# Rotary embedding on one core: float32 from the given tables, x resident in SBUF, plain transfers, and the work shared by VectorE and GpSimd

## Chip, cores, metric

One core of a Trainium2 chip. The metric is device time in microseconds of one execution, lower is better. In the text, HBM is the main memory, SBUF and PSUM are the two memories on the core, VectorE, ScalarE and GpSimd are the engines that compute, and SyncE here only issues transfers. Most executions of one kernel agree within 0.3%.

## The reference

x is 8 x 8 x 1024 x 64 float32 (16.78 MB), the two tables are 1024 x 32 float32 (0.13 MB each).

```python
x_first, x_second = x[..., :32], x[..., 32:]
out_first  = x_first * cos_cached - x_second * sin_cached
out_second = x_first * sin_cached + x_second * cos_cached
```

Everything must be read and written once: 33.56 MB of HBM traffic without the tables. Per output value there are two products and one sum.

## The kernel before

It treats x as 16 spans of 1 MB (128 partitions x 2048 float32). It does not read the tables: it computes sines and cosines on the chip and keeps them as bfloat16. VectorE works in bfloat16. In the first half of the spans ScalarE casts the input and the store casts back; in the second half the load casts and ScalarE casts the output. Casting transfers are issued by GpSimd.

```python
def compute_piece(x16, tt, ot, off, pc):      # all bfloat16, VectorE
    for k in range(2):
        tensor_tensor(out=t4[:, n0:n1, k], in0=x4[:, n0:n1, 1 - k], in1=sinb[:, n0:n1], op=mult)
    tensor_tensor(out=o4[:, n0:n1], in0=x4[:, n0:n1], in1=cb, op=mult)
    tensor_tensor(out=o4[:, n0:n1, 0], in0=o4[..., 0, :], in1=t4[..., 0, :], op=subtract)
    tensor_tensor(out=o4[:, n0:n1, 1], in0=o4[..., 1, :], in1=t4[..., 1, :], op=add)

def emit_piece_a(...):                        # spans 0 to 7
    nc.scalar.copy(out=x16, in_=xt)           # xt came by a plain load
    compute_piece(...)
    nc.gpsimd.dma_start(out=dst, in_=ot)      # bfloat16 -> float32 in the transfer

def emit_piece_b(...):                        # spans 8 to 15, x16 came by a casting load
    compute_piece(...)
    nc.scalar.copy(out=o32, in_=ot)
    nc.scalar.dma_start(out=dst, in_=o32)     # plain store
# ... table stages, pools and piece sizes cut ...
```

Of the kernel before, what the change touches and what calls it, by code (L numbers as in the profile page):

```python
# [11 lines left out]
def kernel(  # L13
# [7 lines left out]
    nc = tc.nc  # L21
    fp32 = mybir.dt.float32
    bf16 = mybir.dt.bfloat16
    int32 = mybir.dt.int32
    TT = mybir.AluOpType
    AF = mybir.ActivationFunctionType
    P = nc.NUM_PARTITIONS
    PI = float(math.pi)
# [3 lines left out]
    BH = b * h  # L32
    chunk_elems = seq * hd

    T_CH = 4
    n_spans = BH // T_CH
    span_elems = T_CH * chunk_elems
    span_free = span_elems // P
    rpp = span_free // hd
    unit = span_free // T_CH  # L40
    nu = rpp // T_CH

    assert seq % rpp == 0 and (rpp * P) % seq == 0

    xf = x.rearrange("b h s d -> (b h s d)")
    of = out.rearrange("b h s d -> (b h s d)")

    const_pool = ctx.enter_context(tc.tile_pool(name="const", bufs=1))
    x32_pool = ctx.enter_context(tc.tile_pool(name="x32", bufs=6))
    x16_pool = ctx.enter_context(tc.tile_pool(name="x16", bufs=8))  # L50
    t_pool = ctx.enter_context(tc.tile_pool(name="t", bufs=4))
    o_pool = ctx.enter_context(tc.tile_pool(name="o", bufs=5))
    o32_pool = ctx.enter_context(tc.tile_pool(name="o32", bufs=4))

    jj = const_pool.tile([P, half], fp32)
    pb_i = const_pool.tile([P, 1], int32)
    pb_m = const_pool.tile([P, 1], int32)
    pb = const_pool.tile([P, 1], fp32)
    pio2 = const_pool.tile([P, 1], fp32)
    freq = const_pool.tile([P, half], fp32)  # L60
    sinb = const_pool.tile([P, rpp, half], bf16)
    cosb = const_pool.tile([P, rpp, half], bf16)
    nj_t = const_pool.tile([P, rpp * half], fp32)
    an_t = const_pool.tile([P, rpp * half], fp32)
    t_t = const_pool.tile([P, rpp * half], fp32)
    ki_t = const_pool.tile([P, rpp * half], int32)
    ar_t = const_pool.tile([P, rpp * half], fp32)

    nc.gpsimd.iota(pb_i, [[1, 1]], base=0, channel_multiplier=rpp)  # L69
    nc.gpsimd.iota(jj, [[1, half]], base=0, channel_multiplier=0,  # L70
                   allow_small_or_imprecise_dtypes=True)
    nc.gpsimd.memset(pio2, PI / 2)
    nc.vector.tensor_scalar(out=pb_m, in0=pb_i, scalar1=seq - 1, scalar2=None,  # L73
                            op0=TT.bitwise_and)
    nc.vector.tensor_copy(out=pb, in_=pb_m)  # L75
    nc.scalar.activation(out=freq, in_=jj, func=AF.Exp, bias=0.0,  # L76
                         scale=float(-math.log(10000.0) / half))

    def emit_table_stage(n0, n1):
        nn = n1 - n0  # L80
        e0, e1 = n0 * half, n1 * half
        nj = nj_t[:, e0:e1]
        an = an_t[:, e0:e1]
        nc.gpsimd.iota(nj.rearrange("p (n j) -> p n j", j=half),  # L84
                       [[1, nn], [0, half]], base=n0,
                       channel_multiplier=0, allow_small_or_imprecise_dtypes=True)
        freq_b = dataclasses.replace(
            freq, ap=[list(freq.ap[0]), [0, nn], list(freq.ap[1])])
        nc.vector.scalar_tensor_tensor(  # L89
            out=an.rearrange("p (n j) -> p n j", j=half),  # L90
            in0=nj.rearrange("p (n j) -> p n j", j=half),
            scalar=pb[:, 0:1], in1=freq_b, op0=TT.add, op1=TT.mult)
        for (shift, tbl) in ((0.0, sinb), (PI / 2, cosb)):
            t = t_t[:, e0:e1]
            ki = ki_t[:, e0:e1]
            arg = ar_t[:, e0:e1]
            nc.vector.tensor_scalar(out=t, in0=an, scalar1=shift,  # L97
                                    scalar2=1.0 / (2 * PI), op0=TT.add, op1=TT.mult)
            nc.vector.tensor_copy(out=ki, in_=t)  # L99
            nc.vector.scalar_tensor_tensor(out=arg, in0=ki, scalar=-2 * PI,  # L100
                                           in1=an, op0=TT.mult, op1=TT.add)
            bias = 0.0 if shift == 0.0 else pio2[:, 0:1]
            nc.scalar.activation(out=tbl[:, n0:n1], in_=arg.rearrange(  # L103
                "p (n j) -> p n j", j=half), func=AF.Sin, bias=bias, scale=1.0)

    cosb4 = dataclasses.replace(
        cosb, ap=[list(cosb.ap[0]), list(cosb.ap[1]), [0, 2], list(cosb.ap[2])])

    def compute_piece(x16, tt, ot, off, pc):
        n0, n1 = off * nu, (off + pc) * nu  # L110
        x4 = x16.rearrange("p (n k j) -> p n k j", k=2, j=half)
        t4 = tt.rearrange("p (n k j) -> p n k j", k=2, j=half)
        o4 = ot.rearrange("p (n k j) -> p n k j", k=2, j=half)
        for k in range(2):
            nc.vector.tensor_tensor(  # L115
                out=t4[:, n0:n1, k, :], in0=x4[:, n0:n1, 1 - k, :],
                in1=sinb[:, n0:n1, :], op=TT.mult)
        cb = dataclasses.replace(
            cosb4, ap=[cosb4.ap[0], [cosb4.ap[1][0], n1 - n0], cosb4.ap[2], cosb4.ap[3]],
            offset=cosb4.offset + n0 * cosb4.ap[1][0])  # L120
        nc.vector.tensor_tensor(out=o4[:, n0:n1], in0=x4[:, n0:n1], in1=cb, op=TT.mult)  # L121
        nc.vector.tensor_tensor(out=o4[:, n0:n1, 0, :], in0=o4[:, n0:n1, 0, :],  # L122
                                in1=t4[:, n0:n1, 0, :], op=TT.subtract)
        nc.vector.tensor_tensor(out=o4[:, n0:n1, 1, :], in0=o4[:, n0:n1, 1, :],  # L124
                                in1=t4[:, n0:n1, 1, :], op=TT.add)

    def emit_piece_a(xt, x16, tt, ot, dst, off, pc):
        fr0, fr1 = off * unit, (off + pc) * unit
        nc.scalar.copy(out=x16[:, fr0:fr1], in_=xt[:, fr0:fr1])  # L129
        compute_piece(x16, tt, ot, off, pc)  # L130
        nc.gpsimd.dma_start(out=dst[:, fr0:fr1], in_=ot[:, fr0:fr1])  # L131

    def emit_piece_b(x16, tt, ot, o32, dst, off, pc):
        fr0, fr1 = off * unit, (off + pc) * unit
        compute_piece(x16, tt, ot, off, pc)
        nc.scalar.copy(out=o32[:, fr0:fr1], in_=ot[:, fr0:fr1])  # L136
        nc.scalar.dma_start(out=dst[:, fr0:fr1], in_=o32[:, fr0:fr1])

    def span_arrs(i):
        base = i * span_elems  # L140
        src = xf[base:base + P * span_free].rearrange("(p m) -> p m", p=P)
        dst = of[base:base + P * span_free].rearrange("(p m) -> p m", p=P)
        return src, dst

    nh = n_spans // 2

    src0, dst0 = span_arrs(0)
    xt0 = x32_pool.tile([P, span_free], fp32, name="xt")
# [74 lines left out]
```

## Time and profile before

| | before |
|---|---|
| time, median of 3 | 90.06 us (90.05 to 90.18) |
| span of the profile that the prediction read | 89.7 us |
| busy: VectorE, ScalarE, GpSimd | 75%, 41%, 15% |
| three DMA queues together | 97.4% of 16 engines' span |

The span runs from the first instruction to the last one on the core. "DMA" in the slices is the mean busy share of the 16 DMA engines in tenths, "GB/s" what they moved.

### The profile page before, as it was taken

The page shows a single profiled execution, that of the slowest core. Times are in us where ns is not written, and L with a number is a line of the kernel's source. Part 1 is how long each engine was busy: PE and PEld are TensorE (multiplying, and loading weights), DVE is VectorE, ACT ScalarE, POOL GpSimd, SP SyncE. Part 2 cuts the span into 40 slices and gives each one's busy share as a digit, 9 for nine tenths or more (in the row PEclk, how much of TensorE's full clock was granted, in tenths as well). Part 3 has the DMA queues.
Part 4 walks back from the last instruction along what each step waited for, and adds up shares of the span by engine and source line. Part 5 has one row for each costly group of instructions (what it writes and reads, how often), then busy time and mean ns, then how long its engine had stood idle before and what let it go on. Part 6 is the DMA issues. An engine that isn't in the chain of part 4 may idle for free.

```text
span 89.7 us, 286 instructions
## 1 busy us (share of the span) xinstructions
DVE 67.0 (75%) x133; ACT 36.4 (41%) x31; POOL 13.0 (15%) x31
## 2 busy tenths in 40 slices
DVE  1000898999999999999999495735959999999000
ACT  5133499989985000000000614400616285747200
POOL 7000000050420420201409722000000000000000
DMA  1999999999998499999599999999999999999991
GB/s 32 246 371 426 427 420 420 438 424 365 389 415 294 184 354 186 416 427 362 208 446 177 331 312 236 316 309 332 318 216 254 339 265 348 405 427 422 409 381 48
DMA packets 6049, 29.37 MB, mean 327 GB/s; under 512 B 672, under 2 KB 928, under 8 KB 3616
## 3 DMA queue, kind: packets, MB, share of 16 engines
q0 software_dynamic: 3024, 12.58, 50.3%
q1 hardware_dynamic: 1440, 8.39, 24.3%
q10 hardware_dynamic: 1584, 8.39, 22.8%
q14 instruction: 1, 0.01, 0.0%
HBM read 16.78 MB, written 16.78 MB: 374 GB/s over the span
## 4 chain that ended last, share of the span: by engine, by line
DVE 35%; DMA 29%; issue 16%; POOL 6%; ACT 5%; SPq 1%; DVEq 0%; POOLq 0%
DMA x<-in_x_dram 19%; DVE tt L115 11%; DMA xt<-in_x_dram 9%; DVE ot L121 9%; DVE ot L122 6%; DVE ot L124 6%; POOL out_dram L131 4%; POOL x L187 2%; ACT x L129 2%; DVE ar_t L100 2%; ACT L103 1%; ACT o L136 1%; ACT sinb L103 0%; SPq L155 0%; SPq L158 0%
## 5 line engine op out<-in xcount | busy, mean ns | idle before, releaser
L136 ACT CAST o<-ot 128x2048 f32<-128x2048 bf16 (+2 forms) x11 | 15.8, 1433 | 39.5 <-DVE ot L124 39.3
L115 DVE TENSOR_TENSOR tt<-x,sinb 128x1024 bf16<-128x1024 bf16 (+2 forms) x44 | 23.3, 540 | 6.3 <-DMA x<-in_x_dram 6.3
L121 DVE TENSOR_TENSOR ot<-x,cosb 128x2048 bf16<-128x2048 bf16 (+2 forms) x22 | 20.2, 928 | 0.0
L129 ACT CAST x<-xt 128x2048 bf16<-128x2048 f32 (+2 forms) x11 | 15.4, 1427 | 6.4 <-DMA xt<-in_x_dram 6.4
L122 DVE TENSOR_TENSOR ot<-ot,tt 128x1024 bf16<-128x1024 bf16 (+2 forms) x22 | 11.8, 540 | 0.1
L124 DVE TENSOR_TENSOR ot<-ot,tt 128x1024 bf16<-128x1024 bf16 (+2 forms) x22 | 11.8, 539 | 0.0
L131 POOL DMA_DIRECT2D out_dram<-ot x11 | 6.0, 545 | 38.4 <-DVE ot L124 38.4
L89 DVE SCALAR_TENSOR_TENSOR an_t<-nj_t,pb,freq 128x256 f32<-128x256 f32 (+1 forms) x3 | 1.6, 570 | 8.1 <-ACT freq L76 8.1
L187 POOL DMA_DIRECT2D x<-in_x_dram x7 | 3.7, 540 | 0.0
L100 DVE SCALAR_TENSOR_TENSOR ar_t<-ki_t,an_t 128x256 f32<-128x256 int32 (+1 forms) x6 | 3.0, 508 | 0.3 <-ACT sinb L103 0.3
L184 POOL DMA_DIRECT2D x<-in_x_dram x3 | 1.6, 537 | 2.6 <-DMA out_dram<-ot 2.0
L99 DVE CAST ki_t<-t_t 128x256 int32<-128x256 f32 (+1 forms) x6 | 1.9, 332 | 0.0
L97 DVE TENSOR_SCALAR t_t<-an_t 128x256 f32<-128x256 f32 (+1 forms) x6 | 1.9, 331 | 0.0
L103 ACT ACTIVATE cosb<-ar_t,pio 128x256 bf16<-128x256 f32 (+1 forms) x3 | 1.6, 573 | 0.4 <-DVE ar_t L100 0.4
L129 ACT ACT_TABLE_LOAD x1 | 1.3, 1283 | 0.7 <-PEq L207 0.7
L103 ACT ACTIVATE sinb<-ar_t 128x256 bf16<-128x256 f32 (+1 forms) x3 | 1.3, 476 | 0.0
L103 ACT ACT_TABLE_LOAD x1 | 1.3, 1283 | 0.0
L84 POOL IOTA nj_t<- 128x256 f32 (+1 forms) x3 | 1.3, 449 | 0.0
L73 DVE TENSOR_SCALAR pb_m<-pb_i 128x1 int32<-128x1 int32 x1 | 0.2, 154 | 1.0 <-POOL pb_i L69 1.0
L76 ACT ACTIVATE freq<-jj 128x32 f32<-128x32 f32 x1 | 0.2, 224 | 0.0
L69 POOL IOTA pb_i<- 128x1 int32 x1 | 0.1, 123 | 0.4 <-PEq L218 0.4
L75 DVE CAST pb<-pb_m 128x1 f32<-128x1 int32 x1 | 0.2, 153 | 0.0
(6 smaller groups left out, 0.6 us busy)
## 6 DMA issues: line engine op xcount, KB each, us to landing
xt<-in_x_dram SPq DMA_DIRECT2D x7, 1024.0 KB, 13.7
out_dram<-ot POOLq DMA_DIRECT2D x6, 1024.0 KB, 5.0
out_dram<-o ACTq DMA_DIRECT2D x6, 1024.0 KB, 8.0
x<-in_x_dram POOLq DMA_DIRECT2D x7, 512.0 KB, 13.2
out_dram<-ot POOLq DMA_DIRECT2D x3, 512.0 KB, 5.1
out_dram<-o ACTq DMA_DIRECT2D x3, 512.0 KB, 5.6
xt<-in_x_dram SPq DMA_DIRECT2D x2, 256.0 KB, 3.7
xt<-in_x_dram SPq DMA_DIRECT2D x1, 512.0 KB, 6.5
```

What stands on the lines that cost most here:

```text
L97: nc.vector.tensor_scalar(out=t, in0=an, scalar1=shift, scalar2=1.0 / (2 * PI), op0=TT.add, op1=TT.mult)
L99: nc.vector.tensor_copy(out=ki, in_=t)
L100: nc.vector.scalar_tensor_tensor(out=arg, in0=ki, scalar=-2 * PI, in1=an, op0=TT.mult, op1=TT.add)
L103: nc.scalar.activation(out=tbl[:, n0:n1], in_=arg.rearrange("p (n j) -> p n j", j=half), func=AF.Sin, bias=bias, scale=1.0)
L115: nc.vector.tensor_tensor(out=t4[:, n0:n1, k, :], in0=x4[:, n0:n1, 1 - k, :], in1=sinb[:, n0:n1, :], op=TT.mult)
L121: nc.vector.tensor_tensor(out=o4[:, n0:n1], in0=x4[:, n0:n1], in1=cb, op=TT.mult)
L122: nc.vector.tensor_tensor(out=o4[:, n0:n1, 0, :], in0=o4[:, n0:n1, 0, :], in1=t4[:, n0:n1, 0, :], op=TT.subtract)
L124: nc.vector.tensor_tensor(out=o4[:, n0:n1, 1, :], in0=o4[:, n0:n1, 1, :], in1=t4[:, n0:n1, 1, :], op=TT.add)
L129: nc.scalar.copy(out=x16[:, fr0:fr1], in_=xt[:, fr0:fr1])
L131: nc.gpsimd.dma_start(out=dst[:, fr0:fr1], in_=ot[:, fr0:fr1])
L136: nc.scalar.copy(out=o32[:, fr0:fr1], in_=ot[:, fr0:fr1])
L187: nc.gpsimd.dma_start(out=x16, in_=src)
```

## The change

The intent: use the given tables in float32, make every transfer plain (no cast, none issued by GpSimd), keep all of x in SBUF and rotate it in place, and split the 16 chunks between VectorE and GpSimd. VectorE's tables and its second product lie in PSUM, so that it has at most one SBUF input and does not compete with GpSimd's reads. Cut to its core:

```diff
-    # tables computed on the chip, bfloat16; casts on ScalarE; casting transfers on GpSimd
+    nc.scalar.dma_start(out=cs[0:Q], in_=cos_cached...)          # Q = 32 partitions
+    nc.scalar.dma_start(out=sn[0:Q], in_=sin_cached...)
+    for c in range(n_ch):                                        # 16 chunks of 1 MB
+        nc.sync.dma_start(out=xt[c], in_=xf[c])
+    for r in range(reps):                                        # 4 groups of 32 partitions
+        nc.scalar.copy(out=csp[r * Q:(r + 1) * Q], in_=cs[0:Q])  # PSUM
+        nc.vector.tensor_copy(out=snp[r * Q:(r + 1) * Q], in_=sn[0:Q])
+    for r in range(1, reps):
+        nc.gpsimd.tensor_copy(out=cs[r * Q:(r + 1) * Q], in_=cs[0:Q])
+    for r in range(1, reps):
+        nc.gpsimd.tensor_copy(out=sn[r * Q:(r + 1) * Q], in_=sn[0:Q])
+    def rotate(eng, q, c, n0, n1, t1, t2, ctab, stab):
+        eng.tensor_tensor(out=a, in0=xr, in1=tab(ctab, n0, n1), op=TT.mult)
+        eng.tensor_tensor(out=s, in0=xr, in1=tab(stab, n0, n1), op=TT.mult)
+        eng.tensor_tensor(out=xr[:, :, 0], in0=a[:, :, 0], in1=s[:, :, 1], op=TT.subtract)
+        eng.tensor_tensor(out=xr[:, :, 1], in0=a[:, :, 1], in1=s[:, :, 0], op=TT.add)
+        q.dma_start(out=of[c]..., in_=xt[c]...)
+    # on_vector: tables csp, snp and product s in PSUM, stores on ScalarE's queue
+    # on_pool:   tables cs, sn and both products in SBUF, stores on SyncE's queue
+    pool_chunks = (1, 4, 7, 10, 13)                              # the other ten: VectorE
+    on_pool(15, 16, R); on_vector(15, 0, 8); on_vector(15, 8, 16)   # last chunk, by rows
```

More of the change, by code (lines that the diff above doesn't have):

```diff
@@ L2 @@
-import dataclasses
-import math
 from contextlib import ExitStack
@@ L7 @@
 import concourse.tile as tile
-from concourse import bass_utils, mybir
+from concourse import mybir
 from concourse._compat import with_exitstack
@@ L22 @@
     fp32 = mybir.dt.float32
-    bf16 = mybir.dt.bfloat16
-    int32 = mybir.dt.int32
     TT = mybir.AluOpType
-    AF = mybir.ActivationFunctionType
     P = nc.NUM_PARTITIONS
-    PI = float(math.pi)
     b, h, seq, hd = x.shape
     half = hd // 2
-    BH = b * h
-    chunk_elems = seq * hd
-    T_CH = 4
-    n_spans = BH // T_CH
-    span_elems = T_CH * chunk_elems
-    span_free = span_elems // P
-    rpp = span_free // hd
-    unit = span_free // T_CH
-    nu = rpp // T_CH
-    assert seq % rpp == 0 and (rpp * P) % seq == 0
@@ L45 @@
-    xf = x.rearrange("b h s d -> (b h s d)")
-    of = out.rearrange("b h s d -> (b h s d)")
-    const_pool = ctx.enter_context(tc.tile_pool(name="const", bufs=1))
-    x32_pool = ctx.enter_context(tc.tile_pool(name="x32", bufs=6))
-    x16_pool = ctx.enter_context(tc.tile_pool(name="x16", bufs=8))
-    t_pool = ctx.enter_context(tc.tile_pool(name="t", bufs=4))
-    o_pool = ctx.enter_context(tc.tile_pool(name="o", bufs=5))
-    o32_pool = ctx.enter_context(tc.tile_pool(name="o32", bufs=4))
-    jj = const_pool.tile([P, half], fp32)
@@ L56 @@
-    pb_i = const_pool.tile([P, 1], int32)
-    pb_m = const_pool.tile([P, 1], int32)
-    pb = const_pool.tile([P, 1], fp32)
-    pio2 = const_pool.tile([P, 1], fp32)
-    freq = const_pool.tile([P, half], fp32)
-    sinb = const_pool.tile([P, rpp, half], bf16)
-    cosb = const_pool.tile([P, rpp, half], bf16)
-    nj_t = const_pool.tile([P, rpp * half], fp32)
-    an_t = const_pool.tile([P, rpp * half], fp32)
-    t_t = const_pool.tile([P, rpp * half], fp32)
-    ki_t = const_pool.tile([P, rpp * half], int32)
@@ L67 @@
-    ar_t = const_pool.tile([P, rpp * half], fp32)
-    nc.gpsimd.iota(pb_i, [[1, 1]], base=0, channel_multiplier=rpp)
-    nc.gpsimd.iota(jj, [[1, half]], base=0, channel_multiplier=0,
-                   allow_small_or_imprecise_dtypes=True)
-    nc.gpsimd.memset(pio2, PI / 2)
-    nc.vector.tensor_scalar(out=pb_m, in0=pb_i, scalar1=seq - 1, scalar2=None,
-                            op0=TT.bitwise_and)
-    nc.vector.tensor_copy(out=pb, in_=pb_m)
-    nc.scalar.activation(out=freq, in_=jj, func=AF.Exp, bias=0.0,
-                         scale=float(-math.log(10000.0) / half))
@@ L79, in emit_table_stage @@
-    def emit_table_stage(n0, n1):
-        nn = n1 - n0
-        e0, e1 = n0 * half, n1 * half
-        nj = nj_t[:, e0:e1]
-        an = an_t[:, e0:e1]
-        nc.gpsimd.iota(nj.rearrange("p (n j) -> p n j", j=half),
-                       [[1, nn], [0, half]], base=n0,
-                       channel_multiplier=0, allow_small_or_imprecise_dtypes=True)
-        freq_b = dataclasses.replace(
-            freq, ap=[list(freq.ap[0]), [0, nn], list(freq.ap[1])])
-        nc.vector.scalar_tensor_tensor(
-            out=an.rearrange("p (n j) -> p n j", j=half),
-            in0=nj.rearrange("p (n j) -> p n j", j=half),
-            scalar=pb[:, 0:1], in1=freq_b, op0=TT.add, op1=TT.mult)
-        for (shift, tbl) in ((0.0, sinb), (PI / 2, cosb)):
-            t = t_t[:, e0:e1]
-            ki = ki_t[:, e0:e1]
-            arg = ar_t[:, e0:e1]
-            nc.vector.tensor_scalar(out=t, in0=an, scalar1=shift,
-                                    scalar2=1.0 / (2 * PI), op0=TT.add, op1=TT.mult)
-            nc.vector.tensor_copy(out=ki, in_=t)
-            nc.vector.scalar_tensor_tensor(out=arg, in0=ki, scalar=-2 * PI,
-                                           in1=an, op0=TT.mult, op1=TT.add)
-            bias = 0.0 if shift == 0.0 else pio2[:, 0:1]
-            nc.scalar.activation(out=tbl[:, n0:n1], in_=arg.rearrange(
-                "p (n j) -> p n j", j=half), func=AF.Sin, bias=bias, scale=1.0)
@@ L106 @@
-    cosb4 = dataclasses.replace(
-        cosb, ap=[list(cosb.ap[0]), list(cosb.ap[1]), [0, 2], list(cosb.ap[2])])
-    def compute_piece(x16, tt, ot, off, pc):
-        n0, n1 = off * nu, (off + pc) * nu
-        x4 = x16.rearrange("p (n k j) -> p n k j", k=2, j=half)
-        t4 = tt.rearrange("p (n k j) -> p n k j", k=2, j=half)
-        o4 = ot.rearrange("p (n k j) -> p n k j", k=2, j=half)
-        for k in range(2):
-            nc.vector.tensor_tensor(
-                out=t4[:, n0:n1, k, :], in0=x4[:, n0:n1, 1 - k, :],
-                in1=sinb[:, n0:n1, :], op=TT.mult)
-        cb = dataclasses.replace(
-            cosb4, ap=[cosb4.ap[0], [cosb4.ap[1][0], n1 - n0], cosb4.ap[2], cosb4.ap[3]],
-            offset=cosb4.offset + n0 * cosb4.ap[1][0])
-        nc.vector.tensor_tensor(out=o4[:, n0:n1], in0=x4[:, n0:n1], in1=cb, op=TT.mult)
-        nc.vector.tensor_tensor(out=o4[:, n0:n1, 0, :], in0=o4[:, n0:n1, 0, :],
-                                in1=t4[:, n0:n1, 0, :], op=TT.subtract)
-        nc.vector.tensor_tensor(out=o4[:, n0:n1, 1, :], in0=o4[:, n0:n1, 1, :],
-                                in1=t4[:, n0:n1, 1, :], op=TT.add)
@@ L127, in emit_piece_a @@
-    def emit_piece_a(xt, x16, tt, ot, dst, off, pc):
-        fr0, fr1 = off * unit, (off + pc) * unit
-        nc.scalar.copy(out=x16[:, fr0:fr1], in_=xt[:, fr0:fr1])
-        compute_piece(x16, tt, ot, off, pc)
-        nc.gpsimd.dma_start(out=dst[:, fr0:fr1], in_=ot[:, fr0:fr1])
-    def emit_piece_b(x16, tt, ot, o32, dst, off, pc):
-        fr0, fr1 = off * unit, (off + pc) * unit
-        compute_piece(x16, tt, ot, off, pc)
-        nc.scalar.copy(out=o32[:, fr0:fr1], in_=ot[:, fr0:fr1])
-        nc.scalar.dma_start(out=dst[:, fr0:fr1], in_=o32[:, fr0:fr1])
@@ L139, in span_arrs @@
-    def span_arrs(i):
-        base = i * span_elems
-        src = xf[base:base + P * span_free].rearrange("(p m) -> p m", p=P)
-        dst = of[base:base + P * span_free].rearrange("(p m) -> p m", p=P)
-        return src, dst
-    nh = n_spans // 2
-    src0, dst0 = span_arrs(0)
-    xt0 = x32_pool.tile([P, span_free], fp32, name="xt")
-    x16_0 = x16_pool.tile([P, span_free], bf16, name="x16")
-    tt0 = t_pool.tile([P, span_free], bf16, name="tt")
-    ot0 = o_pool.tile([P, span_free], bf16, name="ot")
@@ L152 @@
-    nc.sync.dma_start(out=xt0[:, 0:unit], in_=src0[:, 0:unit])
-    emit_table_stage(0, nu)
-    emit_piece_a(xt0, x16_0, tt0, ot0, dst0, 0, 1)
-    nc.sync.dma_start(out=xt0[:, unit:2 * unit], in_=src0[:, unit:2 * unit])
-    emit_table_stage(nu, 2 * nu)
-    emit_piece_a(xt0, x16_0, tt0, ot0, dst0, 1, 1)
-    nc.sync.dma_start(out=xt0[:, 2 * unit:], in_=src0[:, 2 * unit:])
-    emit_table_stage(2 * nu, rpp)
-    emit_piece_a(xt0, x16_0, tt0, ot0, dst0, 2, 2)
-    for i in range(1, nh):
-        src, dst = span_arrs(i)
-        xt = x32_pool.tile([P, span_free], fp32, name="xt")
-        x16 = x16_pool.tile([P, span_free], bf16, name="x16")
-        tt = t_pool.tile([P, span_free], bf16, name="tt")
-        ot = o_pool.tile([P, span_free], bf16, name="ot")
-        nc.sync.dma_start(out=xt, in_=src)
-        pieces = [2, 2] if i == 1 else [T_CH]
-        off = 0
-        for pc in pieces:
-            emit_piece_a(xt, x16, tt, ot, dst, off, pc)
-            off += pc
@@ L175 @@
-    for i in range(nh, n_spans):
-        src, dst = span_arrs(i)
-        x16 = x16_pool.tile([P, span_free], bf16, name="x16")
-        tt = t_pool.tile([P, span_free], bf16, name="tt")
-        ot = o_pool.tile([P, span_free], bf16, name="ot")
-        o32 = o32_pool.tile([P, span_free], fp32, name="o32")
-        if i == n_spans - 1:
-            for (off, pc) in ((0, 2), (2, 1), (3, 1)):
-                fr0, fr1 = off * unit, (off + pc) * unit
-                nc.gpsimd.dma_start(out=x16[:, fr0:fr1], in_=src[:, fr0:fr1])
-                emit_piece_b(x16, tt, ot, o32, dst, off, pc)
-        else:
-            nc.gpsimd.dma_start(out=x16, in_=src)
-            pieces = [2, 2] if i == n_spans - 2 else [T_CH]
-            off = 0
-            for pc in pieces:
-                emit_piece_b(x16, tt, ot, o32, dst, off, pc)
-                off += pc
+    R = 32
@@ new lines @@
+    F = R * hd
+    T = R * half
+    Q = seq // R
+    reps = P // Q
+    n_ch = (b * h * seq) // (R * P)
+    assert seq % R == 0 and P % Q == 0 and Q % 32 == 0
+    xf = x.rearrange("b h s d -> (b h s d)").rearrange(
+        "(c p m) -> c p m", p=P, m=F)
+    of = out.rearrange("b h s d -> (b h s d)").rearrange(
+        "(c p m) -> c p m", p=P, m=F)
+    const = ctx.enter_context(tc.tile_pool(name="const", bufs=1))
+    xp = ctx.enter_context(tc.tile_pool(name="xp", bufs=1))
+    tv = ctx.enter_context(tc.tile_pool(name="tv", bufs=2))
@@ new lines @@
+    tg = ctx.enter_context(tc.tile_pool(name="tg", bufs=1))
+    pt = ctx.enter_context(
+        tc.tile_pool(name="pt", bufs=1, space=bass.MemoryType.PSUM))
+    cs = const.tile([P, T], fp32, name="cs")
+    sn = const.tile([P, T], fp32, name="sn")
+    csp = pt.tile([P, T], fp32, name="csp")
+    snp = pt.tile([P, T], fp32, name="snp")
+    nc.scalar.dma_start(out=cs[0:Q], in_=cos_cached.rearrange("(p n) j -> p (n j)", p=Q))
+    nc.scalar.dma_start(out=sn[0:Q], in_=sin_cached.rearrange("(p n) j -> p (n j)", p=Q))
@@ new lines @@
+    xt = [xp.tile([P, F], fp32, name=f"x{c}") for c in range(n_ch)]
+    for c in range(n_ch):
[7 more added lines that the diff above has]
+        nc.gpsimd.tensor_copy(out=sn[r * Q:(r + 1) * Q], in_=sn[0:Q])
@@ new lines, in rows, with tab @@
+    def rows(t, n0, n1):
+        return t[:, n0 * hd:n1 * hd].rearrange("p (n k j) -> p n k j", k=2, j=half)
+    def tab(t, n0, n1):
+        v = t[:, n0 * half:n1 * half].rearrange("p (n o j) -> p n o j", o=1, j=half)
+        return v.to_broadcast([P, n1 - n0, 2, half])
+    def rotate(eng, q, c, n0, n1, t1, t2, ctab, stab):
+        xr, a, s = rows(xt[c], n0, n1), rows(t1, n0, n1), rows(t2, n0, n1)
+        eng.tensor_tensor(out=a, in0=xr, in1=tab(ctab, n0, n1), op=TT.mult)
+        eng.tensor_tensor(out=s, in0=xr, in1=tab(stab, n0, n1), op=TT.mult)
+        eng.tensor_tensor(out=xr[:, :, 0], in0=a[:, :, 0], in1=s[:, :, 1], op=TT.subtract)
+        eng.tensor_tensor(out=xr[:, :, 1], in0=a[:, :, 1], in1=s[:, :, 0], op=TT.add)
+        q.dma_start(out=of[c][:, n0 * hd:n1 * hd], in_=xt[c][:, n0 * hd:n1 * hd])
@@ new lines, in on_vector, with on_pool @@
+    def on_vector(c, n0=0, n1=R):
+        a = tv.tile([P, F], fp32, name="va")
+        s = pt.tile([P, F], fp32, name="vs")
+        rotate(nc.vector, nc.scalar, c, n0, n1, a, s, csp, snp)
+    def on_pool(c, n0=0, n1=R):
+        a = tg.tile([P, F], fp32, name="ga")
+        s = tg.tile([P, F], fp32, name="gs")
+        rotate(nc.gpsimd, nc.sync, c, n0, n1, a, s, cs, sn)
+    pool_chunks = (1, 4, 7, 10, 13)
+    for c in range(n_ch - 1):
+        if c in pool_chunks:
+            on_pool(c)
+        else:
+            on_vector(c)
@@ L196 @@
+    c = n_ch - 1
+    on_pool(c, 16, R)
+    on_vector(c, 0, 8)
+    on_vector(c, 8, 16)
 _INS = ['x', 'cos_cached', 'sin_cached']
```

## The prediction

> **What bounds the kernel now.** I read the page first: busy shares, the slices, the DMA queues, then the groups with shapes kept apart, then the windows.
>
> ```profile
> DVE 67.0 (75%) x133; ACT 36.4 (41%) x31; POOL 13.0 (15%) x31
> ...
> DMA  1999999999998499999599999999999999999991
> GB/s 32 246 371 426 427 420 420 438 424 365 389 415 294 184 354 186 416 427 362 208 446 177 331 312 236 316 309 332 318 216 254 339 265 348 405 427 422 409 381 48
> ...
> q0 software_dynamic: 3024, 12.58, 50.3%
> q1 hardware_dynamic: 1440, 8.39, 24.3%
> q10 hardware_dynamic: 1584, 8.39, 22.8%
> ...
> HBM read 16.78 MB, written 16.78 MB: 374 GB/s over the span
> ```
>
> No compute engine is near its limit (VectorE 75%), but the 16 DMA engines are busy in nearly every slice, and the three queues' shares add up to 97.4% of 16 engines' span. So the transfers set the time. They move 33.56 MB of HBM traffic, the reference's minimum; only their rate can improve. q0 is the GpSimd-issued queue, whose transfers also cast between float32 and bfloat16: 16.78 MB of HBM traffic (8.39 each way; the page counts 12.58) in 50.3% x 89.7 = 45.1 us of all engines, 372 GB/s. The plain queues do 8.39 MB in 21.8 us (385 GB/s, slow start included) and in 20.5 us (410 GB/s).
>
> The windows show the same in time. Columns: stretch, length, busy us of each engine, clock, DMA share, GB/s.
>
> ```profile
> 4.00:16.00 12.00, 6.23 (x22) 7.77 (x10) 0.00 (x0) 1.00 1.00 406
> ...
> 22.00:50.00 28.00, 27.97 (x44) 6.00 (x4) 8.03 (x16) 1.00 1.00 318
> 50.00:76.00 26.00, 19.62 (x30) 10.49 (x6) 2.06 (x4) 1.00 1.06 299
> 76.00:84.00 8.00, 6.84 (x22) 5.27 (x6) 0.00 (x0) 1.00 1.01 419
> ```
>
> Plain float32 loads alone run at 406 GB/s, plain stores alone at 419; the middle, with casting transfers, shows 299 to 318 although the engines are as busy (part of the drop is only that casts are counted at their smaller side). The ends cost about 2 us before the first packets, and about 2 us between the last heavy slice and the span's end.
>
> **What the Trainium skill says.** (1) "DMA: Bandwidth & Descriptors", section "Measured": a 16 MB load ran at 425 GB/s against about 436 at the fabric; the best slices here (420 to 438) agree. (2) "VectorE: DVE Perf Modes", section "The perf-mode tier table": a two-input elementwise operation runs at twice the base rate in bfloat16 and at the base rate in float32 or with any PSUM operand. The bfloat16 half agrees with this trace: 2048 elements start 1.14 us apart, or 0.53 ns per element plus 0.07 us. No float32 one with two tensors lies in the trace alone to check the other. (3) "SBUF — State Buffer", section "Who interferes with whom": a VectorE instruction with two SBUF inputs contends with GpSimd reads; one with at most one does not. This explains the tables and one product in PSUM. The old trace cannot show it: GpSimd computes nothing there beyond index generation. (4) "GPSIMD Engine Reference", section 3.1: an addition of two 2048-element float32 tensors takes 4497 ns. No row here checks that.
>
> ```profile
> L115 DVE TENSOR_TENSOR tt<-x,sinb 128x1024 bf16<-128x1024 bf16 x24 | 16.3, 686 | 6.3 <-DMA x<-in_x_dram 6.3
> L121 DVE TENSOR_TENSOR ot<-x,cosb 128x2048 bf16<-128x2048 bf16 x12 | 14.6, 1219 | 0.0
> ...
> L129 ACT CAST x<-xt 128x1024 bf16<-128x1024 f32 x3 | 3.0, 1043 | 3.5 <-DMA xt<-in_x_dram 3.5
> ```
>
> **The change, part by part.**
>
> *Removed:* the sine/cosine computation (first product only at 14.7 us in the timeline), both ScalarE casts (about 31 us, beside other work), and all casting DMA. *Added to DMA:* 0.26 MB of tables. Total 33.56 + 0.26 = 33.82 MB. At 413 GB/s, the middle of 406 and 419, that is 81.9 us; with 2 + 2 us for the ends, 85.9 us. This is the DMA floor.
>
> *Start.* By semaphore increments in the old trace, a first 0.25 MB issued at 0.74 us lands between 3.2 and 4.3 us over the engines, and later megabytes every 2.48 us. I put the two tables at 4.5 and 5.2 us (they share the engines with x), x's first chunk at 6, the second at 8.5. ScalarE then makes four PSUM copies of 1024 elements (1.04 us each by its row, plus the waits that the compiled order shows between them): done about 9. VectorE makes four at about 1.2 us from 5.2: done about 10.2 us. GpSimd makes six copies; at 1.0 us each (the 512-element index generation takes 0.62) from 4.5 this would be 10.5, but different partition groups may overlap: I take 9.8.
>
> *VectorE, 10.5 of 16 chunks.* Per chunk two products of 2048 at the base rate and two sums of 1024. Base rate is twice the 0.53 ns: 2048 / 0.96 = 2.13 + 0.07 = 2.20 us; 1024: 1.07 + 0.07 = 1.14. Sum 2 x 2.20 + 2 x 1.14 = 6.68; the order has one self-wait directly behind its producer per chunk, 0.08 us (as the last L122 of the old trace after its L121), and I add 0.08 for PSUM: 6.84. Ten chunks 68.4; the two quarter chunks about 2.0 each: 72.4. End at 10.2 + 72.4 = 82.6. The last 256 KB store then takes about 2.7 us and the span ends 0.85 us after the last landing (88.87 against 89.71 in the old trace): 86.2.
>
> *GpSimd, 5.5 chunks.* 2 x 4.50 + 2 x 2.30 = 13.6 us each, 74.8 in all: end at 84.6; its 512 KB store about 3.2 us, 0.85 more: 88.7.
>
> *Loads* are all issued early, x is never overwritten by another chunk, so compute should wait for data only at the start. Stores come at 1.05 MB per 6.84 us and per 13.6 us, 231 GB/s together, beside the loads on the same DMA engines. GpSimd's stores stand behind all loads in SyncE's order; loads should be through about 60 us, after which some 3 MB of backlog drain within 15 us. The DMA should have slack at the end.
>
> **The path to the end** thus moves from DMA to the later of VectorE (86.2 us span) and GpSimd (88.7), with DMA at 85.9 just behind. Timed runs stood 0.35 us over the span before (90.06 against 89.71), giving 86.5, 89.0 and 86.2. I choose 87.8: the kernel's hand-picked split (a half chunk to GpSimd, the rest in two short stores on VectorE) suggests its author saw the two end together, and GpSimd not late, so I take 1.2 us off the GpSimd sum that rests on a page's figure.
>
> **Rivals.**
> 1. *GpSimd is the end.* If a product takes the page's 4.5 us and waits between dependent GpSimd instructions add 0.3 us a chunk, and the copies run to 11 us, it ends at 11 + 76.5 = 87.5, and the time is 91.9: same or slower. For it: the largest sum of the three. Against: the chosen split. A cold start of GpSimd's library could add to this; the old trace shows such a configuration instruction at 11 ns.
> 2. *DMA stays the bound.* Loads and stores mixed might run below 406; at 390 GB/s (close to the mean of the two plain queues' 385 and 410) 33.82 MB take 86.7 + 4 + 0.35 = 91.1 us: same. For it: DMA is the bound now, and no stretch of the old trace has plain loads beside plain stores. Against: the stretch from 16 to 22 us, mixed, shows 411.
> 3. *PSUM operands or port sharing slow VectorE.* 5% on VectorE gives 3.6 us more, 90 us.
> 4. *GpSimd faster than the page* (4.1 us a product): all three end at 86, a gain of 4 to 5%.
>
> **Range and chances.** The three sums span 86.2 to 89.0; rival 4 and early data take one to two us off, rivals 1 to 3 add two to four: 84.8 to 92.0. Faster by over 2% means below 88.26, just above my value: 0.50. Within 2%: 0.36. Slower (above 91.86), if rivals 1 and 2 come together or GpSimd is well slower than the page: 0.14.
>
> **What would show it right or wrong.** The DMA slices should be full to about 70 us at 400 or more, and fall off after. VectorE rows: 2.2 to 2.3 us for 2048, 1.15 to 1.2 for 1024, first product near 10 us. GpSimd spacing: about 4.5 and 2.3 us, no wait for x after the first chunk. The chain that ended last should run back through GpSimd or VectorE products, not through a load. Wrong would be: VectorE waiting for x in the middle; mixed DMA under 390 GB/s; GpSimd rows far from 4.5 us; VectorE rows stretched while GpSimd runs.

## The result

| | before | after |
|---|---|---|
| time, median of 4 runs | 90.12 us (90.05 to 90.27) | 93.13 us (93.00 to 93.21) |
| ratio | | 1.0318, 95% interval 1.0282 to 1.0354 |
| span of a fast execution | 88.4 us (profiled again later) | 91.1 us |

A ratio here is the mean time of one kernel's fast runs over that of the other's of the same rounds, so not quite the ratio of the medians quoted. The changed kernel is 3.2% slower, and its time lies above the predicted range.

The page of the changed kernel: busy shares, slices, totals.

```profile
DVE 76.3 (84%) x52; ACT 5.3 (6%) x5; POOL 81.5 (89%) x34
...
POOL 0079999999999999999999999999999999999940
DMA  3899999999999999999999999999999911949963
GB/s 54 259 365 358 424 410 432 424 406 435 424 414 435 421 435 424 432 424 417 432 428 435 424 432 424 414 435 428 435 421 435 421 47 47 414 173 410 403 246 149
...
HBM read 17.04 MB, written 16.78 MB: 371 GB/s over the span
```

The DMA engines are no longer busy to the end. They run at 406 to 435 GB/s from 9 until about 73 us and then have holes (two slices of 47). GpSimd (the row POOL) is now busy in nearly every slice. The windows say it in numbers; columns are stretch, length, busy us of VectorE, ScalarE and GpSimd, clock, DMA share, GB/s.

```profile
16.00:40.00 24.00, 23.89 (x14) 0.00 (x0) 23.69 (x9) 1.00 1.01 425
40.00:71.00 31.00, 30.83 (x20) 0.00 (x0) 30.69 (x9) 1.00 1.01 427
71.00:80.00 9.00, 8.97 (x7) 0.00 (x0) 8.92 (x4) 1.00 0.52 218
```

Loads and stores mixed run at 425 to 427 GB/s, where the kernel before had 299 to 318 by the page's count in its middle. That count takes a casting load at its bfloat16 size. In the fast profile of experiment 8 the same stretches show 336 and 300, and with the casting loads' packets counted as float32 373 and 420, together 396, so the rate rose by about 8%. To that extent this part of the intent was met. From 71 to 80 us the DMA engines are half idle while both compute engines are busy all the time. The groups, one shape a row, with busy time and mean ns of one:

```profile
L76 DVE TENSOR_TENSOR vs<-x,snp 128x2048 f32<-128x2048 f32 x10 | 23.0, 2296 | 0.3
L75 DVE TENSOR_TENSOR va<-x,csp 128x2048 f32<-128x2048 f32 x10 | 22.8, 2279 | 0.0
L76 POOL TENSOR_TENSOR gs<-x,sn 128x2048 f32<-128x2048 f32 x5 | 22.6, 4516 | 0.0
L75 POOL TENSOR_TENSOR ga<-x,cs 128x2048 f32<-128x2048 f32 x5 | 22.6, 4515 | 0.4
...
L78 POOL TENSOR_TENSOR x<-ga,gs 128x1024 f32<-128x1024 f32 x5 | 11.7, 2332 | 0.0
L77 POOL TENSOR_TENSOR x<-ga,gs 128x1024 f32<-128x1024 f32 x5 | 11.6, 2324 | 0.4
```

The chain that ended last, in order of time (start, length, what):

```profile
1.17 7.08 DMA sn<-in_sin_cached_dram
...
11.58 4.51 POOL ga L75
...
86.35 1.21 POOL x L78
```

So the end is set thus: GpSimd copies the two tables to its other partitions, begins its first product at 11.58 us, and works without a real pause until 87.56. Its last store and the program's end take 3.56 us more. The chain names the sine table, which landed at 8.26 us, because it came last, but by little: the cosine table landed at 4.94, and GpSimd was busy with its three copies of it until 8.17. The start thus rests on the cosine's landing and on six copies in a row (from the timeline):

```profile
4.99 3.18 POOL L62 COPY cs<-cs 32x1024 f32<-32x1024 f32 x3 [4.55 <-DMA cs<-in_cos_cached_dram]
...
8.31 3.18 POOL L64 COPY sn<-sn 32x1024 f32<-32x1024 f32 x3
```

### The profile page after: what moved, and what is told of

The parts are those of the page before. It is cut to its first block, busy times and chain, and to the rows that moved or that the text cites. A ratio compares the mean times of both kernels' runs of the same rounds, so it can differ in the third digit from the quotient of the medians.

```text
span 91.1 us, 196 instructions
## 1 busy us (share of the span) xinstructions
DVE 76.3 (84%) x52; ACT 5.3 (6%) x5; POOL 81.5 (89%) x34
## 4 chain that ended last, share of the span: by engine, by line
POOL 84%; DMA 8%; issue 2%; POOLq 2%; ACTq 0%
POOL ga L75 27%; POOL gs L76 27%; POOL x L78 14%; POOL x L77 13%; DMA sn<-in_sin_cached_dram 8%; POOL sn L64 3%; POOLq L126 1%; ACTq L51 0%; POOLq L75 0%
## 5 line engine op out<-in xcount | busy, mean ns | idle before, releaser
L75 POOL TENSOR_TENSOR ga<-x,cs 128x2048 f32<-128x2048 f32 (+1 forms) x6 | 24.9, 4155 | 0.5
L76 POOL TENSOR_TENSOR gs<-x,sn 128x2048 f32<-128x2048 f32 (+1 forms) x6 | 24.9, 4155 | 0.0
L76 DVE TENSOR_TENSOR vs<-x,snp 128x2048 f32<-128x2048 f32 (+1 forms) x12 | 24.4, 2029 | 0.4
L75 DVE TENSOR_TENSOR va<-x,csp 128x2048 f32<-128x2048 f32 (+1 forms) x12 | 24.1, 2012 | 0.0
L77 POOL TENSOR_TENSOR x<-ga,gs 128x1024 f32<-128x1024 f32 (+1 forms) x6 | 12.9, 2146 | 0.5
L77 DVE TENSOR_TENSOR x<-va,vs 128x1024 f32<-128x1024 f32 (+1 forms) x12 | 13.0, 1080 | 0.0
L78 DVE TENSOR_TENSOR x<-va,vs 128x1024 f32<-128x1024 f32 (+1 forms) x12 | 12.9, 1079 | 0.0
L78 POOL TENSOR_TENSOR x<-ga,gs 128x1024 f32<-128x1024 f32 (+1 forms) x6 | 12.9, 2152 | 0.0
L60 DVE COPY snp<-sn 32x1024 f32<-32x1024 f32 x4 | 4.9, 1222 | 8.4 <-DMA sn<-in_sin_cached_dram 8.3
L62 POOL COPY cs<-cs 32x1024 f32<-32x1024 f32 x3 | 3.1, 1032 | 4.6 <-DMA cs<-in_cos_cached_dram 4.5
L59 ACT COPY csp<-cs 32x1024 f32<-32x1024 f32 x4 | 4.0, 1008 | 2.1 <-DMA cs<-in_cos_cached_dram 2.0
L64 POOL COPY sn<-sn 32x1024 f32<-32x1024 f32 x3 | 3.1, 1033 | 0.2
```

What stands on the lines that cost most here:

```text
L59: nc.scalar.copy(out=csp[r * Q:(r + 1) * Q], in_=cs[0:Q])
L60: nc.vector.tensor_copy(out=snp[r * Q:(r + 1) * Q], in_=sn[0:Q])
L62: nc.gpsimd.tensor_copy(out=cs[r * Q:(r + 1) * Q], in_=cs[0:Q])
L64: nc.gpsimd.tensor_copy(out=sn[r * Q:(r + 1) * Q], in_=sn[0:Q])
L75: eng.tensor_tensor(out=a, in0=xr, in1=tab(ctab, n0, n1), op=TT.mult)
L76: eng.tensor_tensor(out=s, in0=xr, in1=tab(stab, n0, n1), op=TT.mult)
```

## The experiments

All spans below are of the profiled execution; where rounds were run, the ratio is given. "Gap" is the time of the profiled run minus its span. A run without a ratio is one execution whose state is unknown.

### 1. The sine table first

```diff
-    nc.scalar.dma_start(out=sn[0:Q], in_=sin_cached...)
+    nc.sync.dma_start(out=sn[0:Q], in_=sin_cached...)      # ahead of the loads of x
```

> The sine table goes ahead of x on SyncE's queue instead of second on ScalarE's. Theory A (GpSimd's chain sets the end, and began late because the sine table landed at 8.2 us behind x): both tables land by about 4.5 us, GpSimd's first product starts at about 10.6 instead of 11.6 us, the whole chain and the span move by the same 1 us (91.1 to 90.1), and VectorE starts about 3.5 us earlier without helping. Rival B (DMA or the last stores set the end): the span does not move though GpSimd starts earlier.

Measured: correct, span 90.1, time 92.17 us; ratio to before 1.0187 (1.0117 to 1.0258). Its timeline (start, length, engine, instruction):

```profile
3.74 4.99 DVE L60 COPY snp<-sn 32x1024 f32<-32x1024 f32 x4 [3.74 <-DMA sn<-in_sin_cached_dram]
...
4.08 3.18 POOL L62 COPY cs<-cs 32x1024 f32<-32x1024 f32 x3 [3.64 <-DMA cs<-in_cos_cached_dram]
...
10.58 4.52 POOL L75 TENSOR_TENSOR ga<-x,cs 128x2048 f32<-128x2048 f32 x1
```

The sine table lands at 3.72 instead of 8.26 us, and the cosine table, now with no load of x issued before 1.18 us instead of 0.74, at 4.03 instead of 4.94. GpSimd's first product starts 1.00 us earlier, the span ends 1.05 us earlier. VectorE starts 4.4 us earlier (8.77 against 13.18) and gains nothing for the span. Theory A holds in its main part: GpSimd's chain is the end, and a microsecond at its start is a microsecond at the end. Its reason for the late start does not: 0.91 of the 1.00 us come from the cosine, on which GpSimd waits first, and only about 0.1 from the sine.

### 2. Eight rows from GpSimd to VectorE

```diff
-    on_pool(c, 16, R);  on_vector(c, 0, 8);   on_vector(c, 8, 16)
+    on_pool(c, 24, R);  on_vector(c, 0, 16);  on_vector(c, 16, 24)
```

> Eight rows of the last chunk move from GpSimd to VectorE. Theory A (GpSimd alone is the end): GpSimd ends 8 x 0.43 = 3.4 us earlier (84.1), VectorE 1.7 later (about 86.9), and the span falls by about 0.7 to 1.2 us, VectorE's last store being the end. Rival (VectorE equally late already, or a DMA backlog at the end): no gain or a loss.

Measured: correct, span 91.2, time 93.35 us; ratio to before 1.0316 (1.0256 to 1.0377), no better than without the edit (1.0318). From its timeline:

```profile
83.81 0.72 POOL L78 TENSOR_TENSOR x<-ga,gs 128x256 f32<-128x256 f32 x1
...
86.40 0.41 DVE L78 TENSOR_TENSOR x<-va,vs 128x256 f32<-128x256 f32 x1
```

GpSimd ends at 84.53, 3.0 us earlier; VectorE ends at 86.81, 1.66 later, and is now the end of the chain. The span does not fall, since the tail after the last product grows from 3.56 to 4.4 us. In the trace VectorE's 512 KB and 256 KB stores follow each other within 1.5 us onto DMA engines that are busy just then; that this lengthens the tail was not tested. The size of the gain in theory A was a miss. The two engines were within 2.4 us of balance; shifting rows alone cannot help, only an earlier start or less work can.

### 3. Padding VectorE's instruction stream

The time of the changed kernel stood 2.0 us over its span, where the prediction had taken 0.35. The trace shows an 8 KB instruction transfer after the last instruction, at 93.0 us; the kernel before had one at 24.4 us.

```diff
+    pad = const.tile([P, 128], fp32, name="pad")
+    for i in range(96):
+        nc.vector.memset(pad[:, i:i + 1], 0.0)    # while VectorE waits for the tables
```

> 96 one-element memsets of a scratch tile on VectorE while it waits for the tables, nothing else. The timed 93.1 us stand 2.0 us over the span of 91.1, where the kernel before stands 0.35 over its own. Theory F (an instruction block has to be fetched at the program's end, since the new kernel has few instructions; the trace shows an 8 KB instruction transfer after the end where the kernel before had one at 24.7 us): if VectorE is the engine, the gap falls from 2.0 to about 0.4 us while the span stays 91 to 91.5. Rival G (the gap comes from GpSimd computing, or from PSUM): the gap stays 2.0.

Measured: correct, span 91.1, time 92.89 us, gap 1.77. The instruction transfer moved to 7.6 us, but the gap fell by only 0.25 us. A late instruction transfer goes with 0.2 to 0.3 us (gaps 2.02, 1.94 and 2.06 in the three kernels that show one at the end, 1.77 or 1.78 in nine others; runs 9 and 13 have 2.18 and 2.17 without one at the end, which stays open). It does not explain the rest.

### 4. Transfers only

```diff
-    # table copies, rotate, on_vector, on_pool
+    for c in range(n_ch):
+        q = nc.sync if c in (1, 4, 7, 10, 13) else nc.scalar
+        q.dma_start(out=of[c], in_=xt[c])          # wrong result on purpose
```

> Wrong result on purpose: loads and stores of the changed kernel without any computing (x is written back as it is). The transfers' own floor: theory A expects a span of 82 to 86 us, well under 91, as the slices showed 410 to 435 GB/s with loads and stores mixed; a DMA bound would show 89 or more. For the gap between time and span: theory F (few instructions) expects about 2 us here too; rival G (GpSimd computing or PSUM causes it) expects 0.4.

Measured: span 84.5, time 86.27 us, gap 1.78. Its windows, columns as before without VectorE and ScalarE:

```profile
16.00:40.00 24.00, 0.00 (x0) 1.00 1.01 427
40.00:71.00 31.00, 0.00 (x0) 1.00 1.01 427
```

The transfers of the changed kernel need 84.5 us of span, 6.6 less than it takes and 3.9 less than the 88.4 of the kernel before. So the plain transfers did lower the DMA floor, if the span of the kernel before is taken as its own floor (its queues fill 98.0% of it; no run took the computing out of that kernel); the changed kernel does not reach the new one. The gap is 1.78 us without any computing, so GpSimd computing or PSUM do not cause it.

### 5 to 7. What the gap goes with

```diff
# gp_touch: the changed kernel
-    nc.scalar.dma_start(out=cs[0:Q], in_=cos_cached...)
+    nc.gpsimd.dma_start(out=cs[0:Q], in_=cos_cached...)
# no_tables: transfers only, without the two table loads (wrong result on purpose)
# before_tables: the kernel before, plus
+    nc.sync.dma_start(out=tabs[:, 0], in_=cos_cached...)   # read by nobody
+    nc.sync.dma_start(out=tabs[:, 1], in_=sin_cached...)
```

> The changed kernel with one transfer, the cosine table, issued by GpSimd instead of ScalarE. The padding run and the transfers-only run refuted an instruction fetch and GpSimd computing as the cause of the 1.8 to 2.0 us between span and time. Theory H (a kernel in which GpSimd issues no transfer pays it; the kernel before had 22 such): the gap falls to about 0.4 us here. Rival I (it goes with reading the two tables as further inputs): it stays near 2.0. The span should stay within 1 us of 91.1 either way.

> Wrong result on purpose: the transfers-only kernel without the two table loads. Theory I (the gap of 1.8 us goes with the two further inputs being read): the gap falls to about 0.4 us. Theory H (no transfer issued by GpSimd): it stays at 1.8. The span falls by about 0.6 us from 84.5, the time of 0.26 MB.

> The kernel before, with the two tables loaded into a scratch tile that nobody reads. Theory I (the gap goes with further inputs): the gap rises from 0.35 to about 2 us, the span by about 0.6 us for 0.26 MB more. Theory H: the gap stays at 0.35 us.

Measured: gp_touch span 93.5, gap 1.77; no_tables span 83.4, gap 1.77; before_tables span 89.5, gap 1.77. Neither theory H nor I: the gap was in all three, in the kernel before too. The span of gp_touch was a miss of its own: issued by GpSimd, at 1.24 us and behind x's first loads, the cosine table landed at 8.32 us, GpSimd's first product started at 13.78 instead of 11.58, and the span rose by 2.4. This is the chain of experiment 1 again, in the other direction.

### 8. The kernel before, profiled again

No edit.

> The kernel before, unchanged, profiled anew. In every run since, time stands 1.74 to 2.1 us over the span, and the kernel before ran in two groups, spans 88.0 to 88.9 and 89.7 to 90.7. Theory K (the profile that the prediction read, span 89.7, was of an execution of the slower group, and the prediction joined it to times of the faster group): time minus span is 1.75 us here too, and a fast execution has a span near 88.3. Rival: the kernel before really has a gap of 0.35 us, and this run shows 90.1 us with a span of 89.7.

Measured: time 90.14, span 88.4, gap 1.78. The kernel before ran with spans of 88.0 to 89.2 (fast) and 89.7 to 90.7 (slow), and time stood about 1.8 us over the span in each. Theory K holds, with one step inferred: **the profile that the prediction read was of a slow-group execution, and the prediction set it beside times of the fast group.** The time of that execution is not on record; its span, 89.7, lies at the lower edge of the slow group, and with a gap of 1.77 its time would have been near 91.5 us. The two profiles part early in the chain, first the old one, then the new one:

```profile
2.10 8.48 DMA xt<-in_x_dram
```

```profile
2.11 7.10 DMA xt<-in_x_dram
```

The same load takes 1.38 us longer to land completely in the slow execution. This is one trace of each group, and what makes an execution slow is not shown. The bound is the same in both; the new profile:

```profile
DMA  1999999999999999999699999999999999999990
```

### 9. VectorE's tables in SBUF

```diff
-        rotate(nc.vector, nc.scalar, c, n0, n1, a, s, csp, snp)
+        rotate(nc.vector, nc.scalar, c, n0, n1, a, s, cs, sn)
-    # copies to csp and snp
```

> The changed kernel with VectorE's two tables read from SBUF (the copies that GpSimd uses) instead of PSUM; its second product stays in PSUM. If two SBUF inputs on VectorE contend with GpSimd's reads, the products of both engines stretch: VectorE's 2048-element products from 2.3 us and GpSimd's from 4.5 us, together by several us a chunk, and the span rises from 91.1 to over 100. Rival: no contention, rows stay at 2.2 to 2.3 and 4.5 us and the span stays within 1 us of 91, so that the tables in PSUM buy nothing.

Measured: correct, span 137.4, time 139.63 us. Groups:

```profile
L70 DVE TENSOR_TENSOR va<-x,cs 128x2048 f32<-128x2048 f32 x10 | 50.4, 5044 | 8.1 <-POOL cs L57 8.1
L71 DVE TENSOR_TENSOR vs<-x,sn 128x2048 f32<-128x2048 f32 x10 | 46.0, 4601 | 3.4 <-POOL sn L59 3.1
L71 POOL TENSOR_TENSOR gs<-x,sn 128x2048 f32<-128x2048 f32 x5 | 32.7, 6544 | 0.0
L70 POOL TENSOR_TENSOR ga<-x,cs 128x2048 f32<-128x2048 f32 x5 | 28.4, 5689 | 0.4
```

VectorE's products go from 2.28 and 2.30 to 5.04 and 4.60 us, GpSimd's from 4.52 to 5.69 and 6.54. GpSimd's sums stretch too (2.32 and 2.33 to 4.25 and 3.55), but VectorE's sums, which kept one input in PSUM, stay at 1.21 us. In the timeline a product that overlaps the other engine's takes nearly the time of both, 2.3 and 4.5 us, as if the two took turns:

```profile
35.37 6.62 DVE L71 TENSOR_TENSOR vs<-x,sn 128x2048 f32<-128x2048 f32 x1
39.79 6.54 POOL L71 TENSOR_TENSOR gs<-x,sn 128x2048 f32<-128x2048 f32 x1
41.91 6.58 DVE L70 TENSOR_TENSOR va<-x,cs 128x2048 f32<-128x2048 f32 x1
```

The tables in PSUM are worth 46 us of span; without them the sharing is worse than VectorE alone with its tables in PSUM, as the next run shows.

### 10. VectorE alone

```diff
-    pool_chunks = (1, 4, 7, 10, 13)
+    pool_chunks = ()            # and the last chunk whole on VectorE
```

> GpSimd takes no chunk; VectorE does all 16. If GpSimd does not slow VectorE in the changed kernel, a chunk stays at 6.78 us and the span is about 13.2 + 16 x 6.78 + 4.5 = 126 us, so GpSimd's share buys 35 us. Rival: VectorE speeds up alone (contention was there), to 6.4 us a chunk or less, and the span is 120 or less.

Measured: correct, span 127.2, time 128.98 us.

```profile
L76 DVE TENSOR_TENSOR vs<-x,snp 128x2048 f32<-128x2048 f32 x16 | 36.7, 2296 | 0.5
```

With GpSimd idle after its table copies, VectorE's product takes the same 2296 ns as beside it. So with the tables in PSUM VectorE loses nothing to contention (the port half of rival 3 of the prediction), and GpSimd's share buys 36 us. No run has GpSimd computing alone.

### 11. Plain transfers alone, in the kernel before

```diff
-    nc.gpsimd.dma_start(out=dst..., in_=ot...)          # spans 0 to 7
+    nc.scalar.copy(out=o32..., in_=ot...);  nc.scalar.dma_start(out=dst..., in_=o32...)
-    nc.gpsimd.dma_start(out=x16, in_=src)               # spans 8 to 15
+    nc.sync.dma_start(out=xt, in_=src);     nc.scalar.copy(out=x16, in_=xt)
```

> The plain-transfer part of the change alone, in the kernel before: every load and store float32 and plain on SyncE's and ScalarE's queues, all casts to and from bfloat16 on ScalarE (about 60 us of its time), VectorE's bfloat16 work and computed tables as before. Fast spans of the kernel before are 88.0 to 88.6. If its bound was the casting transfers' rate, the span falls to 84 to 86.5 us (transfers-only without tables: 83.4). Rival: ScalarE's fixed order of casts and stores stalls loads or VectorE, and the span stays at 88 or more.

Measured: correct, span 92.6, time 94.32 us; ratio to before 1.0435 (1.0336 to 1.0533). A window of its middle, then waits of the whole span (engine and line, what ended the wait, us in total, times, longest):

```profile
16.00:60.00 44.00, 35.67 (x61) 33.62 (x23) 0.00 (x0) 1.00 1.01 416
```

```profile
DVE tt L115 <- ACT x L193: 8.5, 2, 4.3
ACT o L138 <- DVE ot L124: 7.9, 8, 2.0
```

The rival holds, and the expected 84 to 86.5 us of span was a miss. The DMA rate did rise to 416 GB/s, but ScalarE now has all casts in one order, and the engines wait for each other: ScalarE for landed stores (four waits between 27 and 38 us, 4.8 us in all; the four output buffers now serve all 16 spans), VectorE for ScalarE's casts (three waits of 3.8 to 4.3 us, which end at 41.8, 57.4 and 79.6). With casting loads counted as float32, the kernel before moved 390 GB/s in the same stretch (run 8), so the rate rose by 7%. That casting transfers kept the rate down is shown to that extent; that removing them alone lowers the time is not shown.

### 12. An earlier start for both engines

```diff
-    nc.scalar.dma_start(out=sn[0:Q], ...)
+    nc.sync.dma_start(out=sn[0:Q], ...)
-        nc.gpsimd.tensor_copy(out=sn[r * Q:(r + 1) * Q], in_=sn[0:Q])
+        nc.scalar.copy(out=sn[r * Q:(r + 1) * Q], in_=sn[0:Q])
-    pool_chunks = (1, 4, 7, 10, 13)
+    pool_chunks = (0, 3, 6, 9, 12)       # chunks 12 to 14 in halves of 16 rows
-    on_pool(c, 16, R);  on_vector(c, 0, 8);   on_vector(c, 8, 16)
+    on_pool(c, 20, R);  on_vector(c, 0, 12);  on_vector(c, 12, 20)
```

> Both tables first, each on its own queue; ScalarE makes GpSimd's three sine copies; GpSimd takes chunk 0, which lands first, and 12 instead of 16 rows of the last chunk; chunks 12 to 14 in halves so that stores come more evenly. Theory A (the lead-in and the compute chains, not DMA, set the span): GpSimd starts at about 7.4 us, ends at about 81.5, VectorE at about 82.2, span about 86 (85.3 to 86.8). Rival: DMA (span of the transfers-only run 84.5) or a tail of backed-up stores keeps it at 88 or more.

Measured: correct, span 86.4, time 88.23 us; ratio to before 0.9813 (0.978 to 0.9847).

```profile
7.26 4.51 POOL L75 TENSOR_TENSOR ga<-x,cs 128x2048 f32<-128x2048 f32 x1
...
81.46 0.98 POOL L78 TENSOR_TENSOR x<-ga,gs 128x384 f32<-128x384 f32 x1
82.16 0.41 DVE L78 TENSOR_TENSOR x<-va,vs 128x256 f32<-128x256 f32 x1
```

GpSimd starts at 7.26 and ends at 82.44, VectorE at 82.57, close to the 81.5 and 82.2 expected. GpSimd starts 4.32 us earlier than in the changed kernel and ends 5.12 earlier; the parts of this edit were not run one by one. By the medians this version is 4.9 us faster than the changed kernel (93.13), and by the ratio it is 1.9% faster than the kernel before: clear of noise, but the interval holds the 2% threshold. It still works in float32 from the given tables.

### 13. Finer last pieces

```diff
-    on_pool(c, 20, R);  on_vector(c, 0, 12);  on_vector(c, 12, 20)
+    on_pool(c, 20, 28); on_pool(c, 28, R)
+    on_vector(c, 0, 12); on_vector(c, 12, 16); on_vector(c, 16, 20)
```

> early_start with the last pieces cut finer: GpSimd's 12 rows as 8 and 4, VectorE's 20 as 12, 4 and 4, so that the last store of each engine is 128 KB instead of 384 and 256 KB. If the size of the last store matters, its landing comes about 0.4 us sooner after the last product and the added instructions cost about 0.3 us on each engine: span 86.2 to 86.6 against 86.4, and a time of 1.8 us more. Rival (the end is backed-up stores on the DMA engines): the span falls by 0.5 us or more.

Measured: correct, span 87.2, time 89.32 us; ratio to before 0.9896 (0.9868 to 0.9923): slower than run 12, and neither the expected span (86.2 to 86.6) nor the rival's fall. The tables landed 0.3 us later in this execution, and the pieces cost about 0.4 us on VectorE and 0.8 on GpSimd. VectorE's last store, half as large, landed 1.96 us after its issue instead of 2.87, but a wait took that back. The end of its timeline:

```profile
82.31 2.29 ACTq L79 DMA_DIRECT2D out_dram<-x  x2
...
82.98 0.28 DVE L78 TENSOR_TENSOR x<-va,vs 128x128 f32<-128x128 f32 x1
```

VectorE's last sum ends at 83.26, but the second of the two stores, 0.34 us long and ending with the row at 84.60, was issued only at 84.26: the compiled order gives it one of eight transfer semaphores whose earlier user, a store of GpSimd's rows on SyncE's queue, landed only at 84.18 (from the trace's semaphore increments). Here more and smaller stores ran into that reuse. The gap of this run was 2.17 us without an instruction transfer at the end (its one of 8 KB came at 73.4 us); this part of the gap's variation stays open.

## Why the prediction was wrong

The prediction chose 87.8 us; measured were 93.13. Its sum for GpSimd was a span of 88.7. Five terms of the sum make up the 5.3 us:

| term, as the prediction put it | predicted | measured | error |
|---|---|---|---|
| time over span ("Timed runs stood 0.35 us over the span") | 0.35 | 2.02 | 1.67 |
| GpSimd's start ("I take 9.8") | 9.8 | 11.58 | 1.78 |
| GpSimd's chunks ("74.8 in all") | 74.8 | 75.98 | 1.18 |
| last store and end (3.2 + 0.85) | 4.05 | 3.56 | -0.49 |
| "I take 1.2 us off the GpSimd sum" | -1.2 | 0 | 1.2 |

The errors add up to 5.34; 87.8 + 5.34 = 93.14, the profiled run's time.

- **Bound of the kernel before: right as far as known.** Both profiles show its DMA engines busy in nearly every slice, and the changed kernel's transfers alone need 3.9 us less; no run took the computing out of the kernel before. Two readings were off. The page counts a cast at its destination (12.58 MB are 8.39 of float32 stores and 4.19 of bfloat16 loads), not at the smaller side, and this is the whole drop to 299 and part of that to 318 (422 and 354 GB/s with float32 sizes). And the stretch from 16 to 22 us, held against rival 2 as mixed, has loads alone: no store's packet runs before 22.5 us.
- **DMA floor: nearly right, and rival 2 refuted.** Predicted 85.9 us of span, measured 84.5 with nothing computed. Mixed loads and stores ran at 425 to 427 GB/s, above the 413 assumed and the 390 of rival 2 (which the prediction called close to the mean of 385 and 410, 397.5).
- **VectorE: durations right, start wrong.** 6.78 us a chunk against 6.84. It started at 13.18 instead of 10.2, since its four copies of the sine table waited for that table's landing at 8.26 instead of 5.2, and ended at 85.15 against 82.6. The prediction said that the tables "share the engines with x", but gave the second only 0.7 us more than the first; it took 3.3. Rival 3 is refuted: its port half by experiment 10, its PSUM half by the 6.78 us. The base rate was right, though its working was not exact: twice 0.53 ns is 2.17 us for 2048 elements, not 2.13.
- **GpSimd: rival 1 came true, and the start failed most.** A product took 4.5 us as "GPSIMD Engine Reference", section 3.1, says of an addition, so rival 4 is refuted. The two waits a chunk added 0.15 us (13.75 against 13.6), and the half chunk took 7.20 us against 6.8. The start came at 11.58 instead of 9.8: the cosine landed at 4.94 instead of 4.5 (0.44), the six copies took 6.50 us with the waits between them instead of 6.0 (0.50), the sine was waited for 0.14, and the overlap of copies for which 0.7 had been taken off did not occur: they ran one after another, 3.18 us for three. Rival 1's 87.5 for GpSimd's end met the measured 87.56 partly by luck: its start at 11 was too early, its wait of 0.3 us a chunk too long.
- **The discount: wrong in kind.** Taking 1.2 us off because the author "saw the two end together" replaced a sum of measured and stated durations by a guess about intent. The two did end 2.4 us apart, both late.
- **The conversion: wrong in kind.** One profile of unknown state was joined to times of other executions. Every kernel profiled with its time stood 1.77 us or more above its span, the kernel before too (experiment 8). The comparison suffered as well: the fast span to beat was 88.4, not 89.7. With 1.77 us of gap and no discount, the prediction's three sums would have been 87.7 (DMA), 88.0 (VectorE) and 90.4 us (GpSimd), and the latest of them is "same", not "faster".

Where did the expected gain go? The transfers alone fell 3.9 us below the span of the kernel before, then an 11.6 us lead-in and 76 us of GpSimd work took their place as the bound. Run 12 shows that part of the gain was there: with the lead-in cut to 7.3 us and the rows shared anew, the span falls to 86.4.

## What to carry to other kernels

When transfers stop being the bound, a microsecond before the first product of the engine that ends last counts in full, until another engine ends last; send small tables ahead of the large loads, and let an idle engine spread them. When VectorE and GpSimd share float32 work of two inputs as here, keep one of VectorE's inputs in PSUM (46 us in run 9), and judge a split by the sums of both chains, not by intent. Before turning a span into a time, check that the profile and the times belong to the same execution, or to the same state.

## What the Trainium skill lacked or had wrong

- "SBUF — State Buffer", section "Who interferes with whom": right that two SBUF inputs on VectorE contend with GpSimd's reads. It gives the rule, an exclusive lock, without durations for a kernel that shares work so: here VectorE's products went from 2.3 to 4.6 and 5.0 us, GpSimd's from 4.5 to 5.7 and 6.5, and the span from 91.1 to 137.4. The 6.5 to 6.6 us of products that overlapped fit such a lock.
- "GPSIMD Engine Reference", section 3.1: its 4497 ns for an addition holds for a product in a whole kernel too (4515 and 4516 ns). The two waits a chunk between dependent instructions, 0.15 us here, are not in it.
- "DMA: Bandwidth & Descriptors", section "Where 436 GB/s comes from": it says that for HBM to SBUF the HBM side at about 358 GB/s binds. With one core running, loads and stores mixed held 425 to 427 GB/s for 55 us, so the sentence does not hold for a core alone; the 425 GB/s that the prediction cites from the same page already differ from it. No run here has two cores at work.
- The same page, section "Queues, rings and completion order": it describes round-robin between queues but gives no landing time for a small transfer beside large loads. A 128 KB table took 7.1 us from issue to landing behind the start of x's loads, and 3.0 us ahead of them.
- No page has the difference met here between the time of an execution and the span of its instructions: 1.77 or 1.78 us in nine of the 14 kernels profiled with their time, and 1.94 to 2.18 in the other five.
